# Layer 0's loop: the second layer's modulation sums are written behind the second and third tile's output projection

## The chip, the cores and the metric

The kernel runs on one core of one Trainium2 chip. The metric is the device time of one execution in microseconds (us). Below, PE is the matrix engine (TensorE), DVE the vector engine, ACT the scalar engine, POOL GpSimd, and SP the engine whose queue issues nearly all the transfers (DMAs).

## What is computed

A two-layer encoder trunk over 2048 positions of 1024 features. Each layer first scales and shifts its input and, at its end, gates what the mixer made, with three vectors (shift, scale, gate) that come from a conditioning vector `c`:

```
cond = silu(c)
for layer in range(2):
    mod = cond @ ada_w[layer] + ada_b[layer]          # 1024 x 3072
    shift, scale, gate = split(mod, 3)
    h = x * (1 + scale) + shift
    y = even_mixer(h) if layer == 0 else odd_mixer(h)
    x = layer_norm(alpha * x + gate * y, ln_g, ln_b)
```

`even_mixer` (layer 0) projects `h` by `ev_w_in` to attention inputs, to the two inputs of a spatial gating unit and to a gate, runs windowed attention and the spatial gating, multiplies by the gate and projects by `ev_w_out`. `odd_mixer` (layer 1) projects by `od_w_in`, convolves, runs two gated recurrences and projects by `od_w_out`.

## The kernel before

The 2048 positions are cut into four tiles of 512 (`NT = 4`, `t` = 0 to 3). Attention comes first, for all tiles (up to about 300 us of the profile). Then a loop over the four tiles finishes layer 0 (about 300 to 900 us), and layer 1 follows. This case is about that loop.

Every product of two matrices is done in three passes: each operand is split into a rounded part and a rest (`split`, lines 154 to 156: ACT writes the rounded part, DVE subtracts), and `mm3` (lines 158 to 161) adds three matmuls. A weight unit is 128 rows by 512 columns of a weight matrix. `wunit` loads it into `raw` (three buffers, SP, line 570), ACT and DVE split it into `hl` (eight buffers, line 155 and line 156), and PE uses it for four matmuls of 512 columns in three passes, twelve in all. So the weights come down a chain SP, DMA, ACT, DVE, PE, and `hl` can run at most eight units ahead of PE. While units pass, `wunit` also calls `prepare`, which loads a piece of layer 1's weights (`praw`), splits it (`phl`) and stores it for later. The pieces of `od_w_out` are also multiplied by layer 1's gate (line 790).

One turn of the loop is:

- `sgate(t)`: four jobs of eight units, with four PSUM banks each: the first (`sv`) ends in statistics on DVE (lines 689 to 700), then the gate job, the `u` job, and a fourth whose result meets the attention output `o`. It gives `y`.
- the modulation sums that `mods` lists for this tile, by `modulation`,
- `load_hT(t + 1)`: eight transfers of 512 KB that bring the next tile's input (`ahi`, `alo`), or for the last tile `build1(0)`, which makes layer 1's first input and needs layer 1's shift and scale,
- `project_out(t, y)`: two jobs of eight units (`n` = 0 and 1). DVE multiplies each result by layer 0's gate (`gz`, line 755), adds it to `z` (line 757), and `norm_rows` normalises and stores four `z` of 128 by 1024 (lines 616 to 627).

`modulation(..., layer, part, n)` makes one half (512 columns) of one of the vectors: part 0 is shift, 1 is scale, 2 is gate. It loads four `aw` of 512 KB (line 174, two buffers), DVE multiplies and adds eight slices of 128x512 into `macc` (line 182 once and line 184 seven times), and PE then adds up the 128 partitions: for a gate by one matmul with ones (line 192), whose result ACT copies to `gate1` (line 193), for shift and scale by DVE copies into `parts` (line 202), eight matmuls of one column (line 206) and a short DVE instruction (line 211 or 213). The list is

```
mods = {0: [(0, 2, 0), (0, 2, 1)], 1: [(1, 2, 0), (1, 2, 1), (1, 0, 0)], 2: [(1, 0, 1), (1, 1, 0), (1, 1, 1)]}
```

so layer 0's own gate is summed in tile 0, layer 1's gate and half of its shift in tile 1, and the rest in tile 2. Layer 1's gate is first used when tile 3 begins, its shift and scale in `build1(0)` after tile 3's `sgate`.

The order on each engine is not the order of the text: a scheduler places the instructions, taking those that stand earlier in the program first where several are ready, and on the chip each engine then takes its own in that order. Where PE meets a matmul of line 192 or 206 whose sum is not there yet, all later matmuls wait.

Of the kernel before, what the change touches and what calls it, by code (L numbers as in the profile page):

```python
# [54 lines left out]
def kernel(  # L55
# [39 lines left out]
    def pool(stack, name, side=None, bufs=1, space=None):  # L95
        kw = {} if space is None else {"space": space}
        if side is not None:
            kw["side"] = side
        return stack.enter_context(tc.tile_pool(name=name, bufs=bufs, reuse_waits="tile", **kw))
# [63 lines left out]
    def bank(p, tag, shape=(128, C)):  # L163
        t = p.tile(list(shape), F32, tag=tag, name=tag)
        return t

    def modulation(mp, pp, tag, layer, part, n, gate=None, wide=None):
        c0 = part * D + n * C
        acc = mp.tile([128, C], F32, tag="macc", bufs=2, name="macc")
        m = mp.m  # L170
        sums = None if wide is None else bank(*pp)
        for k2 in range(KD // m):
            aw = mp.tile([128, m, C], F32, tag=tag, name="aw")
            load(out=aw, in_=ada_w[layer, k2 * m * 128:(k2 + 1) * m * 128, c0:c0 + C].rearrange(
                "(j p) n -> p j n", p=128))
            for j in range(m):
                k = m * k2 + j
                if sums is not None:
                    q = 32 * (k % 4)
                    nc.tensor.matmul(sums[q:q + 32, :], lhsT=wide[:, k], rhs=aw[:, j], start=k < 4, stop=k >= 4)  # L180
                elif k == 0:
                    ts(out=acc, in0=aw[:, j], scalar1=cond[:, 0:1], scalar2=None, op0=ALU.mult)
                else:
                    stt(out=acc, in0=aw[:, j], scalar=cond[:, k:k + 1], in1=acc, op0=ALU.mult, op1=ALU.add)
        if sums is not None:
            act(out=acc, in_=sums, func=AF.Copy)
        ps = bank(*pp)
        if part == 2:
            brow = mp.tile([1, C], F32, tag="brow", bufs=1, name="brow")
            load(out=brow, in_=ada_b[layer:layer + 1, c0:c0 + C])  # L190
            tt(out=acc[0:1, :], in0=acc[0:1, :], in1=brow, op=ALU.add)
            nc.tensor.matmul(ps, lhsT=ones, rhs=acc, start=True, stop=True)
            act(out=gate[:, n * C:n * C + C], in_=ps, func=AF.Copy)
            return
        if layer == 0:
            pr, ks = slice(0, 128), slice(4 * n, 4 * n + 4)
            parts = acc.rearrange("p (k m) -> p k m", k=4)
        else:
            pr, ks = slice(64 * n, 64 * n + 64), slice(0, 8)
            parts = mp.tile([128, 8, 64], F32, tag="parts", bufs=1, name="parts")  # L200
            for a in range(2):
                nc.vector.tensor_copy(parts[:, :, 32 * a:32 * a + 32],
                                      acc[:, 256 * a:256 * a + 256].rearrange("p (k q) -> p k q", k=8))
        w = ks.stop - ks.start
        for k in range(w):
            nc.tensor.matmul(ps[pr, k:k + 1], lhsT=parts[:, k], rhs=ones[:, 0:1], start=True, stop=True)
        dst = (shift, scale)[part][pr, layer, ks]
        v0 = layer * 24 + part * 8
        bias = vcol0[pr, v0 + ks.start:v0 + ks.stop]
        if part == 1:  # L210
            stt(out=dst, in0=ps[pr, 0:w], scalar=1.0, in1=bias, op0=ALU.add, op1=ALU.add)
        else:
            tt(out=dst, in0=ps[pr, 0:w], in1=bias, op=ALU.add)
# [310 lines left out]
    def load_hT(t):  # L524
        hT = ([], [])
        for k2 in range(4):
            hi, lo = act_pair()
            nc.sync.dma_start(out=hi.bitcast(F32), in_=h_d[t][0][:, 2 * k2:2 * k2 + 2, :])
            nc.sync.dma_start(out=lo.bitcast(F32), in_=h_d[t][1][:, 2 * k2:2 * k2 + 2, :])
            for j in range(2):  # L530
                hT[0].append(hi[:, j])
                hT[1].append(lo[:, j])
        return hT
# [24 lines left out]
    pm = pool(sp, "pm", left, bufs=2, space=PSUM)  # L558
# [8 lines left out]
    def wunit(srcs, perm=False):  # L567
        raw = tp.tile([128, C], F32, tag="raw", bufs=3, name="raw")
        for dst, src in srcs(raw):
            r = load(out=dst, in_=src)  # L570
        hl = cp.tile([128, 2, C], F32R, tag="hl", bufs=8, name="hl")
        if perm:
            v = [hl[:, i].rearrange("p (i u d) -> p i u d", u=2, i=4) for i in range(2)]
            split(v[0], v[1], raw.rearrange("p (u i d) -> p i u d", u=2, i=4))
        else:
            split(hl[:, 0], hl[:, 1], raw)
        count[0] += 1
        while todo and count[0] >= todo[0][0]:
            prepare(todo.pop(0)[1], r)
        return hl  # L580
# [23 lines left out]
    def job_tm(unit, hT, order=range(KD)):  # L604
        ps = banks()
        for i, k in enumerate(order):
            hl = unit(k)
            for b in range(4):
                sl = slice(b * 128, b * 128 + 128)
                mm3(ps[b], hT[0][k][:, sl], hT[1][k][:, sl], hl[:, 0], hl[:, 1], i == 0, i == KD - 1)  # L610
        return ps

    def norm_rows(p, z, dst, g_bc, b_bc, parts=1):
        st6 = p.tile([128, 2, 6], F32, tag="st6", bufs=2, name="st6")
        for n in range(2):
            nc.vector.bn_stats(st6[:, n, :], z[:, n * C:n * C + C])
        mv = p.tile([128, 2], F32, tag="mv", bufs=2, name="mv")
        nc.vector.bn_aggr(mv, st6.rearrange("p a b -> p (a b)"))  # L618
        rstd = p.tile([128, 1], F32, tag="rstd", bufs=2, name="rstd")
        rsqrt_eps(rstd, mv[:, 1:2], 1.0)  # L620
        w = D // parts
        for n in range(parts):
            cs = slice(n * w, n * w + w)
            zs = z[:, cs]
            stt(out=zs, in0=zs, scalar=mv[:, 0:1], in1=g_bc[:, cs], op0=ALU.subtract, op1=ALU.mult)
            stt(out=zs, in0=zs, scalar=rstd, in1=b_bc[:, cs], op0=ALU.mult, op1=ALU.add)
            store(out=dst[:, cs], in_=zs)

    sd = ExitStack()
    bp = pool(sd, "sgate", right)  # L630
# [4 lines left out]
    gates = (gate0, gate1)  # L635
# [25 lines left out]
    def out_rows(w, c0):  # L661
        def f(k):
            if k < 4:
                return lambda raw: [(raw[64 * u:64 * u + 64], w[256 * u + 64 * k:256 * u + 64 * k + 64, c0:c0 + C])
                                    for u in range(2)]
            return lambda raw: [(raw, w[k * 128:k * 128 + 128, c0:c0 + C])]
        return f
# [75 lines left out]
    def project_out(t, y):  # L743
        zt = []
        for b in range(4):
            z = bp.tile([128, D], F32, tag="z", bufs=5, name="z")
            load(out=z, in_=xs[t * C + b * 128:t * C + b * 128 + 128, :])
            zt.append(z)
        for n in range(2):
            cw = out_rows(w1, n * C)  # L750
            ps = job_tm(lambda k: wunit(cw(k)), y, (4, 5, 6, 7, 0, 1, 2, 3))
            for b in range(4):
                gz = bp.tile([128, C], F32, tag="gz", bufs=2, name="gz")
                with tc.high_priority():
                    tt(out=gz, in0=ps[b], in1=gate0[:, n * C:n * C + C], op=ALU.mult)  # L755
                zs = zt[b][:, n * C:n * C + C]
                stt(out=zs, in0=zs, scalar=ALPHA, in1=gz, op0=ALU.mult, op1=ALU.add)
        for b in range(4):
            r = t * C + b * 128
            norm_rows(bp, zt[b], x1_d[r:r + 128, :], g_bc, b_bc)  # L760
# [80 lines left out]
    mods = {0: [(0, 2, 0), (0, 2, 1)], 1: [(1, 2, 0), (1, 2, 1), (1, 0, 0)], 2: [(1, 0, 1), (1, 1, 0), (1, 1, 1)]}  # L841
    order = list(range(16, 56)) + list(range(16))
    for t, (i0, i1) in enumerate(((0, 8), (8, 24), (24, 38), (38, 56))):
        for i in range(i0, i1):
            todo.append((48 * t + 48 * (i - i0 + 1) // (i1 - i0), order[i]))
    for t in range(NT):
        y = sgate(t, hT)
        for m in mods.get(t, []):
            modulation(Ring(bp, bp, "aw", 2, 2), (pm, "pm"), "aw", *m, gate=gates[m[0]])
        hT = load_hT(t + 1) if t + 1 < NT else build1(0)  # L850
        project_out(t, y)
        if t == 0:
            vectors1()

# [6 lines left out]
    pm = pool(sa, "pm1", bufs=3, space=PSUM)  # L861
# [368 lines left out]
```

## Time and profile before

| | us |
|---|---|
| median of three runs | 1553.41 (1550.63 to 1558.35) |
| the profiled execution, time | 1552.3 |
| its span (first to last instruction) | 1550.4 |
| PE busy | 1475.9 (95%) |
| DVE busy | 1186.5 (77%) |
| ACT busy | 784.2 (51%) |

The profile gives each engine's busy time over the span, in 40 slices of 38.8 us, and can be asked for single instructions with what they waited for. 1.9 us of the profiled execution lie outside the span. PE is busy nearly throughout, so the questions are where PE stands still, and how far the chain of weight units runs ahead of it at each place.

### The profile page before, as it was taken

How to read it: one execution, taken by the hardware profiler on the slowest of the kernel's cores; microseconds unless marked ns; L12 is line 12 of the kernel's file. 1: busy time of each engine (PE TensorE's matmuls, PEld its weight loads, DVE VectorE, ACT ScalarE, POOL GpSimd, SP SyncE). 2: the span in 40 equal slices, each digit the busy share in tenths (PEclk: the TensorE clock that was granted, in tenths of full speed). 3: DMA queues.
4: the chain of work that ended last, by engine and by line, in shares of the span. 5: the costliest groups of instructions: out<-in, count | busy, mean ns of one | idle time of the engine just before them, and what ended most of it. 6: DMA issues, size and time to landing. Idle time of an engine off the chain costs nothing. (4 is left out here: it accounts for less than half of the span.)

```text
span 1550.4 us, 22105 instructions
## 1 busy us (share of the span) xinstructions
PE 1475.9 (95%) x7096; PEld 1181.1 (76%) x7096; DVE 1186.5 (77%) x2180; ACT 784.2 (51%) x1470; POOL 413.1 (27%) x496
## 2 busy tenths in 40 slices
PE   7999999989999999999999899999999999989997
PEld 3887777657777787788888777778787788877886
DVE  4499898845659576976785875878878857879996
ACT  4677777533422342243242417589498588771110
POOL 1024223212003200210030232444555513214432
PEclk9999999999999999999999999999999999999999
DMA  9367776848788979897795689797787666438862
GB/s 345 131 171 218 214 215 179 268 120 294 237 268 301 254 236 314 317 307 251 254 299 183 200 253 278 245 264 262 243 260 249 230 232 241 165 145 307 280 237 103
DMA packets 208315, 370.91 MB, mean 239 GB/s; under 512 B 55720, under 2 KB 102724, under 8 KB 208200
## 3 DMA queue, kind: packets, MB, share of 16 engines
q1 hardware_dynamic: 201192, 354.52, 70.7%
q0 software_dynamic: 7008, 14.99, 3.8%
q8 instruction: 56, 0.92, 0.2%
q14 instruction: 59, 0.48, 0.1%
HBM read 261.96 MB, written 85.97 MB: 224 GB/s over the span
## 5 line engine op out<-in xcount | busy, mean ns | idle before, releaser
L155 ACT ACTIVATE hl<-raw 128x512 fp32r<-128x512 f32 x192 | 118.7, 627 | 228.6 <-DMA raw<-in_ev_w_in_dram 136.4
L159 PE MATMUL pj<-ahi,hl 128*128 128x512 f32 x512 | 200.4, 394 | 1.1 <-DVE gz L755 1.1
L160 PE MATMUL pj<-alo,hl 128*128 128x512 f32 x512 | 201.2, 393 | 0.0
L161 PE MATMUL pj<-ahi,hl 128*128 128x512 f32 x512 | 200.2, 392 | 0.0
L156 DVE TENSOR_TENSOR hl<-raw,hl 128x512 fp32r<-128x512 f32 x192 | 131.6, 694 | 74.0 <-ACT hl L155 73.9
L151 POOL TENSOR_SCALAR rstd<-mv 128x1 f32<-128x1 f32 x32 | 32.0, 999 | 409.7 <-DVE mv L618 297.3
L159 PEld LDWEIGHTS pj<-ahi,hl 128*128 128x128 f32 x512 | 96.9, 189 | 22.2 <-DVE gz L755 1.5
L160 PEld LDWEIGHTS pj<-alo,hl 128*128 128x128 f32 x512 | 96.8, 189 | 20.5
L161 PEld LDWEIGHTS pj<-ahi,hl 128*128 128x128 f32 x512 | 96.8, 189 | 20.3
L466 POOL DMA_DIRECT2D P<-T x112 | 62.5, 566 | 177.8 <-DVE nm L431 77.6
L159 PE MATMUL pj<-wqh,hhi 128*128 128x256 f32 (+1 forms) x256 | 88.3, 349 | 2.6 <-ACT hhi L155 1.7
L431 DVE CUSTOM_DVE_ANT_0 P<-psc,mask,nsink 128x384 f32<-128x384 f32 (+1 forms) x128 | 73.7, 593 | 21.0 <-PE psc L430 20.9
L155 ACT ACTIVATE phl<-praw 128x512 fp32r<-128x512 f32 x56 | 35.4, 631 | 106.5 <-DMA praw<-in_od_w_in_dram 52.8
L160 PE MATMUL pj<-wql,hhi 128*128 128x256 f32 (+1 forms) x256 | 87.6, 343 | 0.0
L161 PE MATMUL pj<-wqh,hlo 128*128 128x512 f32 (+1 forms) x256 | 85.2, 345 | 1.1 <-DVE hlo L156 1.0
L979 DVE SCALAR_TENSOR_TENSOR ii<-ii,xc 128x1024 f32<-128x1024 f32 (+2 forms) x32 | 40.6, 1269 | 57.9 <-ACT ii L973 57.9
L434 ACT ACTIVATE P<-P,nm 128x384 f32<-128x384 f32 (+1 forms) x128 | 76.4, 601 | 11.4 <-DVE nm L431 11.2
L779 POOL TENSOR_TENSOR alo<-hm,ahi 128x512 fp32r<-128x512 f32 x32 | 48.5, 1523 | 119.1 <-DVE hm L778 115.0
L949 DVE SCALAR_TENSOR_TENSOR xc<-X,vcol,xc 128x512 f32<-128x512 f32 (+2 forms) x96 | 75.2, 817 | 0.3
L159 PE MATMUL pm<-xhi,hg 128*128 128x512 f32 (+3 forms) x160 | 55.4, 361 | 14.3 <-ACT xhi L155 6.5
L156 DVE TENSOR_TENSOR phl<-praw,phl 128x512 fp32r<-128x512 f32 x56 | 39.0, 697 | 34.2 <-ACT phl L155 23.3
L777 ACT ACTIVATE ahi<-hm,shift,scale 128x512 fp32r<-128x512 f32 x32 | 25.2, 811 | 74.4 <-DVE hm L776 67.2
(305 smaller groups left out, 4314.1 us busy)
## 6 DMA issues: line engine op xcount, KB each, us to landing
hl<-w_d SPq DMA_DIRECT2D x128, 512.0 KB, 4.7
raw<-in_ev_w_in_dram SPq DMA_DIRECT2D x128, 256.0 KB, 4.2
w_d<-phl SPq DMA_DIRECT2D x40, 512.0 KB, 4.6
aw<-in_ada_w_dram SPq DMA_DIRECT2D x32, 512.0 KB, 6.0
hg<-w_d SPq DMA_DIRECT2D x32, 512.0 KB, 5.7
P<-T SPq DMA_DIRECT2D x104, 96.0 KB, 4.7
P<-T POOLq DMA_DIRECT2D x104, 96.0 KB, 4.3
aw<-in_ada_w_dram SPq DMA_DIRECT2D x8, 1024.0 KB, 8.2
```

What stands on the lines that cost most here:

```text
L151: nc.gpsimd.tensor_scalar(out=dst, in0=src, scalar1=mul, scalar2=EPS, op0=ALU.mult, op1=ALU.add)
L155: act(out=hi, in_=src, func=AF.Copy)
L156: tt(out=lo, in0=src, in1=hi.bitcast(F32), op=ALU.subtract)
L159: nc.tensor.matmul(ps, lhsT=ahi, rhs=bhi, start=first, stop=False)
L160: nc.tensor.matmul(ps, lhsT=ahi, rhs=blo, start=False, stop=False)
L161: nc.tensor.matmul(ps, lhsT=alo, rhs=bhi, start=False, stop=last)
L431: nc.vector.tensor_tensor_reduce(out=p[:, g, 0:W], in0=ps[:, 0:W], in1=mask[:, m0:m0 + W], scale=-0.125, scalar=nsink[:, h:h + 1], op0=ALU ...
L434: act(out=p[:, g, 0:W], in_=p[:, g, 0:W], func=AF.Exp, scale=-1.0, bias=nm[:, h:h + 1], accum_out=rs[:, h:h + 1])
L466: dma.dma_start(out=pv[32 * r:32 * r + 32, 0:nb, i], in_=T[32 * i:32 * i + 32, 0:nk].rearrange("p (j r) m -> p r j m", r=4)[:, r])
L779: nc.gpsimd.tensor_tensor(out=lo[:, j], in0=h, in1=hi[:, j].bitcast(F32), op=ALU.subtract)
L949: stt(out=xc[:, w], in0=xt[:, j0 + j:j0 + j + W], scalar=vcol1[:, 8 * j + g:8 * j + g + 1], in1=xc[:, w], op0=ALU.mult, op1=ALU.add)
L979: stt(out=ii[i][:, :, w], in0=ii[i][:, :, w], scalar=1.0, in1=xc[:, None, w].to_broadcast([128, 2, W]), op0=ALU.add, op1=ALU.mult)
```

## The change

In tile 0 nothing is changed. In tiles 1 and 2 the call of `modulation` moves from between `sgate` and `load_hT` to behind `project_out`. No instruction is added or removed and no operand changes.

```
+    def later_sums(t):
+        for m in mods.get(t, []):
+            modulation(Ring(bp, bp, "aw", 2, 2), (pm, "pm"), "aw", *m, gate=gates[m[0]])
+
     for t in range(NT):
         y = sgate(t, hT)
-        for m in mods.get(t, []):
-            modulation(Ring(bp, bp, "aw", 2, 2), (pm, "pm"), "aw", *m, gate=gates[m[0]])
+        if t == 0:
+            later_sums(t)
         hT = load_hT(t + 1) if t + 1 < NT else build1(0)
         project_out(t, y)
+        if t > 0:
+            later_sums(t)
         if t == 0:
             vectors1()
```

What this does to the order on the engines, at three places. (A number behind a name tells buffers of one name apart. It differs between the two kernels for the same thing.)

PE, the second half of layer 1's gate (line 192). Before, in tile 1's `project_out`, between the first two units of its second job (banks `px`):

```order
L161 MATMUL px_6274<-hl_6280,alo_5754 128x512
L159 MATMUL px_6275<-hl_6280,ahi_5753 128x512
L160 MATMUL px_6275<-hl_6280,ahi_5753 128x512
L161 MATMUL px_6275<-hl_6280,alo_5754 128x512
L192 MATMUL pm_6031<-macc_6014,ones_138 128x512
L159 MATMUL px_6274<-hl_6297,ahi_5753 128x512
L160 MATMUL px_6274<-hl_6297,ahi_5753 128x512
```

After, near the end of the gate job of tile 2's `sgate` (banks `pja`):

```order
L159 MATMUL pja_6710<-ahi_5999,hl_6817 128x512
L160 MATMUL pja_6710<-alo_6000,hl_6817 128x512
L161 MATMUL pja_6710<-ahi_5999,hl_6817 128x512
L192 MATMUL pm_6465<-macc_6448,ones_138 128x512
L159 MATMUL pja_6711<-ahi_5999,hl_6817 128x512
L160 MATMUL pja_6711<-alo_6000,hl_6817 128x512
L161 MATMUL pja_6711<-ahi_5999,hl_6817 128x512
```

That matmul stands 267 instructions of PE later than before. The other five of lines 192 and 206 that belong to tiles 1 and 2 move back likewise. The matmul of the gate's first half now opens tile 2, while its eight slices on DVE stay where they were.

SP, tile 1, where the next tile's input is loaded. Before, two of the gate's four `aw` stand around the first `ahi` and `alo`:

```order
L174 DMA aw_6023<-in_ada_w_dram 128x2x512
L733 DMA o_7257<-o_d2_68 128x512
L733 DMA o_7266<-o_d2_68 128x512
L528 DMA ahi_6067<-h_d2_0_66 128x1024
L529 DMA alo_6068<-h_d2_1_67 128x1024
L528 DMA ahi_6071<-h_d2_0_66 128x1024
L529 DMA alo_6072<-h_d2_1_67 128x1024
L805 DMA w_d21_117<-phl_6301 128x1024
L174 DMA aw_6027<-in_ada_w_dram 128x2x512
L570 DMA raw_6338<-in_ev_w_out_dram 128x512
```

After, at the same place:

```order
L733 DMA o_7257<-o_d2_68 128x512
L528 DMA ahi_5991<-h_d2_0_66 128x1024
L529 DMA alo_5992<-h_d2_1_67 128x1024
L528 DMA ahi_5995<-h_d2_0_66 128x1024
L529 DMA alo_5996<-h_d2_1_67 128x1024
L805 DMA w_d21_117<-phl_6225 128x1024
L733 DMA o_7266<-o_d2_68 128x512
L570 DMA raw_6262<-in_ev_w_out_dram 128x512
```

The two loads are gone from here. They and the sixteen that follow them move back by some 15 to 18 weight units, into tile 2 and the start of tile 3.

DVE, the last sum (the second half of layer 1's scale). Before, it stands in tile 2's `project_out`, among the splits of its weight units:

```order
L184 SCALAR_TENSOR_TENSOR macc_7349<-aw_7354,cond_140,macc_7349 128x512
L211 SCALAR_TENSOR_TENSOR scale_144<-pm_7336,vcol0_141 64x8
L184 SCALAR_TENSOR_TENSOR macc_7349<-aw_7358,cond_140,macc_7349 128x512 x2
L156 TENSOR_TENSOR hl_7620<-raw_7618,hl_7620 128x512
L156 TENSOR_TENSOR hl_7637<-raw_7635,hl_7637 128x512
L156 TENSOR_TENSOR phl_7641<-praw_7640,phl_7641 128x512
L184 SCALAR_TENSOR_TENSOR macc_7349<-aw_7362,cond_140,macc_7349 128x512 x2
```

After, it stands in the first job of tile 3's `sgate`, among `norm_rows` of tile 2, the statistics of `sv` and the multiplications by `gate1`:

```order
L184 SCALAR_TENSOR_TENSOR macc_7764<-aw_7773,cond_140,macc_7764 128x512
L690 TENSOR_SCALAR mu_7955<-mu_7955 128x8
L690 TENSOR_SCALAR mu_7967<-mu_7967 128x8
L626 SCALAR_TENSOR_TENSOR z_7311<-z_7311,rstd_7698,b_bc_4083 128x1024
L156 TENSOR_TENSOR hl_8143<-raw_8141,hl_8143 128x512
L790 TENSOR_TENSOR praw_8146<-praw_8146,gate1_4085 128x512
L184 SCALAR_TENSOR_TENSOR macc_7764<-aw_7777,cond_140,macc_7764 128x512
L694 TENSOR_TENSOR sv_7958<-pja_7794,mu_7955 128x512
L694 TENSOR_TENSOR sv_7970<-pja_7795,mu_7967 128x512
L790 TENSOR_TENSOR praw_8195<-praw_8195,gate1_4085 128x512
L184 SCALAR_TENSOR_TENSOR macc_7764<-aw_7777,cond_140,macc_7764 128x512
```

All eight slices of that sum, and the copies of two sums into `parts`, now lie between the `gz` of tile 2's second job and the end of tile 3's statistics. The order on POOL is the same in both kernels.

## The prediction

> **What bounds the kernel now.** First the page: span, busy times, and the slices of PE and DVE.
>
> ```profile
> span 1550.4 us, 22105 instructions
> ...
> PE 1475.9 (95%) x7096; PEld 1181.1 (76%) x7096; DVE 1186.5 (77%) x2180; ACT 784.2 (51%) x1470; POOL 413.1 (27%) x496
> ...
> PE   7999999989999999999999899999999999989997
> ...
> DVE  4499898845659576976785875878878857879996
> ```
>
> PE is the bound, with 74.5 us idle in the whole span. A change of order can win only where PE waits, and lose only by new waits. So next I cut the loop that is changed into windows of 20 us. The columns are PE, weight loads, DVE, ACT, POOL (busy us, count), granted clock, DMA share, GB/s.
>
> ```profile
> core 0: us, PE busy (x) PEld busy (x) DVE busy (x) ACT busy (x) POOL busy (x), PEclk, DMA share, GB/s
> ...
> 580.00:600.00 20.00, 16.77 (x66) 12.78 (x65) 11.03 (x19) 3.88 (x7) 0.00 (x0) 0.91 1.00 311
> 600.00:620.00 20.00, 20.00 (x101) 16.46 (x100) 15.92 (x27) 4.95 (x9) 0.00 (x0) 1.00 0.96 319
> 620.00:640.00 20.00, 20.00 (x90) 16.56 (x89) 20.00 (x34) 5.87 (x10) 5.88 (x8) 1.00 0.78 274
> 640.00:660.00 20.00, 18.32 (x81) 14.88 (x80) 20.00 (x36) 6.89 (x12) 4.48 (x5) 1.00 1.02 365
> ...
> 740.00:760.00 20.00, 20.00 (x90) 16.56 (x89) 12.90 (x23) 5.99 (x10) 0.00 (x0) 1.00 0.91 323
> 760.00:780.00 20.00, 20.00 (x90) 16.55 (x89) 20.00 (x33) 6.22 (x10) 6.77 (x7) 1.00 0.62 209
> 780.00:800.00 20.00, 20.00 (x90) 16.57 (x89) 17.89 (x30) 7.28 (x13) 7.29 (x10) 1.00 0.95 320
> 800.00:820.00 20.00, 20.00 (x90) 16.58 (x89) 13.27 (x21) 9.59 (x17) 1.33 (x1) 1.00 0.77 255
> ```
>
> Two windows lose PE time. At 580 to 600 the DMA engines are full (1.00) and the clock drops. At 640 to 660 PE loses 1.7 us, and DVE is full from 620 on. From 760 on DVE is full too, yet PE is not held up there. Third, the timeline of PE gives the waits one by one (in brackets: idle time, and what ended it).
>
> ```profile
> 444.34 1.10 PE L192 MATMUL pm<-macc,ones 128*128 128x512 f32 x2 [2.49 <-DVE macc L191]
> 592.79 1.81 PE L192 MATMUL pm<-macc,ones 128*128 128x512 f32 x2 [3.23 <-DVE macc L191]
> 648.36 0.73 PE L161 MATMUL pjb<-ahi,hl 128*128 128x512 f32 x2 [1.68 <-DVE hl L156]
> ...
> 854.47 0.50 PE L159 MATMUL pja<-hl,ahi 128*128 128x512 f32 x1 [0.88 <-ACT yt L736]
> 877.86 0.50 PE L159 MATMUL pjb<-hl,ahi 128*128 128x512 f32 x1 [1.57 <-DVE gz L755]
> 881.56 0.50 PE L159 MATMUL pjb<-hl,ahi 128*128 128x512 f32 x1 [1.59 <-DVE gz L755]
> 901.05 0.50 PE L159 MATMUL pj<-ahi,hl 128*128 128x512 f32 x1 [1.06 <-DVE gz L755]
> ```
>
> The wait of 444 belongs to tile 0 and stays. The one of 592.79 is the second half of layer 1's gate, which the change moves. Its cause, from the timelines of SP and DVE:
>
> ```profile
> 576.15 0.42 SPq L528 DMA_DIRECT2D ahi<-h_d  x1
> ...
> 579.35 0.66 SPq L174 DMA_DIRECT2D aw<-in_ada_w_dram  x1
> ...
> 581.97 0.74 DVE L184 SCALAR_TENSOR_TENSOR macc<-aw,cond,macc 128x512 f32<-128x512 f32 x1
> 589.25 1.54 DVE L184 SCALAR_TENSOR_TENSOR macc<-aw,cond,macc 128x512 f32<-128x512 f32 x2 [6.54 <-DMA aw<-in_ada_w_dram]
> 591.97 0.67 DVE L191 TENSOR_TENSOR macc<-macc,brow 1x512 f32<-1x512 f32 x1
> ```
>
> The last `aw` of this sum was issued behind the burst of `ahi` and `alo` and took 9.9 us (579.35 to 589.25). DVE stood still for it and for the splits queued behind it, and PE for DVE.
>
> **The change part by part.**
>
> *The wait at 592.79 goes.* It cost more than its 3.23 us: behind it the clock was halved.
>
> ```profile
> 593.00:596.40 3.40, 3.40 (x7) 2.03 (x7) 1.58 (x4) 1.12 (x2) 0.00 (x0) 0.51 1.01 268
> ...
> 445.00:449.00 4.00, 4.00 (x19) 3.12 (x18) 4.00 (x8) 0.59 (x1) 0.00 (x0) 1.00 0.88 275
> ```
>
> 3.40 us at 0.51 lose 3.40 x 0.49 = 1.7 us. After the 2.49 us at 444 the clock stayed at 1.00. So the term is 3.23 + 1.7 = 4.9 us. Without this matmul PE has `hl` units in store there (it was a sum that was missing, no weight unit), and two loads of 512 KB leave the burst. What would be late next is the weights of the same burst: they get earlier, not later.
>
> The Trainium skill, page "TensorE: Matmul & The Clock Gate", section "Part 1: The HAM clock gate", has the clock go to half only after an idle window of about 3.4 us, and the window running free. Read strictly, a gap of 3.23 us holds no whole window; the row of 593 shows that here it sufficed, so the trace disagrees by a little. By the strict rule the term would be 3.23 and the end result 1.7 us later.
>
> *The wait at 648.36 goes for the most part.* It is a weight unit that DVE split too late, some 28 us into the stage in which it is full. What one sum costs DVE, by the instructions on `macc` (duration in ns: least, median, most):
>
> ```profile
> L184 DVE SCALAR_TENSOR_TENSOR macc<-aw,cond,macc x56: 684/746/753, 365.6 to 732.1; 128x512 f32<-128x512 f32 x56
> L182 DVE TENSOR_SCALAR macc<-aw,cond x8: 468/474/485, 364.6 to 714.7; 128x512 f32<-128x512 f32 x8
> ...
> L202 DVE COPY parts<-macc x8: 271/285/295, 617.3 to 733.6; 128x256 f32<-128x256 f32 x8
> ```
>
> And the landing of the `aw` that are issued between 560 and 740 us:
>
> ```profile
> DMA to landing us min/median/max: 3.8/5.4/9.8
> ```
>
> One sum is 0.47 + 7 x 0.746 = 5.7 us, a pair of copies 0.57. Between 600 and 620 a whole sum with its copies leaves DVE (6.3 us, and 2 MB of loads at a DMA share of 0.96). Between 620 and 650 the slices of one sum are replaced by those of another, so the load stays. DVE enters this stage further ahead, but PE comes 4.9 us earlier. Bounds 0 and 1.68; I take 1.2, near the full wait, as the relief of 6.3 us is above the 4.9.
>
> *The six moved matmul places.* Each can hold up PE, bounded by 0 and by the 4.9 us of the worst seen. The gate's first half: its slices on DVE do not move and its matmul now stands 192 instructions of PE later (some 43 us at 90 in 20.00 us), so 0. The second half comes near the end of tile 2's gate job, shift's first half a few units later, each but a few units behind the DVE rows that it needs, while DMA is at 1.02 (640 to 660). The others have a whole job between. I take 1.2 us in all, nearer to 0, since in the loop two of eight such sums waited.
>
> *Tile 3's first job.* DVE gets one sum (5.7), two pairs of copies (1.1) and three short ones (0.3): 7.1 us in a stage that is full. What lies between DVE and PE there: the subtraction of the first job's last unit and its first matmul, and the same for the third job's first unit.
>
> ```profile
> 785.35 0.68 DVE L156 TENSOR_TENSOR hl<-raw,hl 128x512 fp32r<-128x512 f32 x1
> ...
> 793.06 0.68 DVE L694 TENSOR_TENSOR sv<-px,mu 128x512 f32<-128x512 f32 x1
> ...
> 794.66 1.37 DVE L156 TENSOR_TENSOR hl<-raw,hl 128x512 fp32r<-128x512 f32 x2 [0.32 <-ACT hl L155]
> ...
> 789.26 0.39 PE L159 MATMUL pjb<-ahi,hl 128*128 128x512 f32 x1
> ...
> 801.50 0.39 PE L159 MATMUL px<-ahi,hl 128*128 128x512 f32 x1
> ```
>
> The first lead is 789.26 - 786.03 = 3.2 us. Ahead of that subtraction six slices and a pair of copies are put (0.47 + 5 x 0.746 + 0.57 = 4.8), so the unit is 1.6 us late. The second lead is 801.50 - 795.35 = 6.2, against 7.1: 0.9 late, which the first wait already covers. The last `sv` ends at 793.7 + 7.1 = 800.8, in time for the banks at 801.50. DVE may enter further ahead, since the sum has left 715 to 733; but at 740 to 760 it is only 12.90 busy, so it is not what limits the lead, and I count nothing for that. Bounds 0 and 7.1; I take 1.5. Behind it DVE recovers, having 6.7 us free in 800 to 820.
>
> *No cost:* ACT's two copies of the gate move behind matmuls that are earlier in PE's order than the units ACT splits then; with 51% ACT has room. The loads are the same bytes, and the moved ones end before `build1(0)`. Layer 1's order does not change.
>
> Sum: -4.9 - 1.2 + 1.2 + 1.5 = -3.4 us. Against the profiled execution's 1552.3 that is 1548.9. The median of the runs lies 1.1 above that execution, so I predict 1550.
>
> **The rivals.**
>
> *The waits only change place* (the change then does not do what it says: the sums still fall among other matmuls, a third of a tile later). One moved matmul waits as at 592.79, 4.9 us again, beside tile 3's 1.5: 1552.3 - 1.2 + 1.5 = 1552.6, 1553.7 on the median. For it: DMA at 1.02 in 640 to 660, where the second half's loads now fall. Against: the six waited once before, and now most have a job between.
>
> *All waits of the tail close:* the two named (6.6 us) and the four from 854 to 901 (0.88 + 1.57 + 1.59 + 1.06 = 5.1): -11.7, which gives 1540.6, or 1541.7 on the median. For it: PE arrives earlier at them. Against: they are ended by `gz` and `yt`, which follow PE's own results.
>
> *Slower: the last sum's loads come late in tile 3's first job.* DVE takes its instructions in order, and DMA is at 0.95 in 780 to 800. If both its later loads hold DVE as at 589.25, the units are late by 7.1 + 2 x 6.54 - 3.2 = 17.0 us, 18.7 with a slow clock. With the gains of 6.1 that is +12.6: 1564.9, or 1566 on the median. It decides from a lateness of about 6 us on (the gains), and is slower by a measurable amount from 14 us on. Against it: the loads are issued some 5 units ahead of their use, and the median took 5.4 us to land.
>
> **How the numbers follow.** 0.5% is 7.8 us, about what a measurement of this kernel can tell from no change: faster means below 1545.6, slower above 1561.2. The forecast, 1546 to 1553, has a chance of 0.58; the waits that change place, 1552 to 1558, 0.25; all waits closed 0.10; late loads 0.07. Faster is the third case, 0.10. Slower is most of the last, 0.06. The rest, 0.84, cannot be told from no change. The range runs from 1544 (both named waits gone and nothing new, 6.6 us, less a little) to 1558 (the second case, with as much as the highest run shown).
>
> **What would show it.** After: line 192 without a wait near 590 and a clock of 1.00 in 580 to 600; no wait near 648; DVE at 20.00 through 760 to 800, and a wait of 1 to 3 us of PE near 790 ended by `hl` or `sv`. I am wrong if a matmul of line 192 or 206 waits over 3 us at its new place, if DVE waits for `aw` near 790, or if layer 1 takes a different time.

## The result, and the profile after

| | before | after |
|---|---|---|
| median of 17 runs | 1552.56 us | 1561.61 us |
| lowest to highest | 1546.79 to 1560.18 | 1555.81 to 1571.41 |
| the profiled execution, time | 1552.3 | 1563.16 |
| its span | 1550.4 | 1561.4 |

The ratio of after to before is 1.0051, with a 95% interval of 1.0037 to 1.0065. The change makes the kernel slower by some 8 us, where the prediction had 1550 us and called a difference too small to tell the likeliest outcome. The means of the 17 runs, 1561.2 and 1553.2 us, are 8.0 us apart. One run of one kernel below (the new place with neither loads nor wide slices), at a granted clock of 0.848 and 1631.59 us, is left out of its ratio.

The page of the changed kernel, the lines that answer to those of before:

```profile
span 1561.4 us, 22109 instructions
...
PE 1483.7 (95%) x7096; PEld 1184.9 (76%) x7096; DVE 1186.6 (76%) x2180; ACT 782.5 (50%) x1470; POOL 417.7 (27%) x496
...
PE   7899999899999998999999999999999999989997
```

PE has the same number of matmuls and is busy 7.8 us longer (1483.7 against 1475.9). A matmul at half clock counts as busy for longer (0.63 us instead of 0.39 behind the wait near 593 before), so a part of the loss must be granted clock. The other engines do as many instructions in nearly the same time (POOL 417.7 us against 413.1). The four instructions more in all (22109 against 22105) are semaphore waits, which count on no engine. The windows of 20 us over the changed loop show where it falls (columns as before: PE, weight loads, DVE, ACT, POOL, granted clock, DMA share, GB/s):

```profile
580.00:600.00 20.00, 15.83 (x63) 12.33 (x63) 8.54 (x15) 5.13 (x9) 0.00 (x0) 0.91 0.80 253
600.00:620.00 20.00, 19.17 (x83) 15.18 (x81) 7.65 (x14) 4.82 (x9) 0.00 (x0) 1.00 0.84 275
620.00:640.00 20.00, 19.35 (x85) 15.91 (x86) 20.00 (x34) 5.05 (x9) 5.41 (x6) 1.00 0.61 193
640.00:660.00 20.00, 19.53 (x85) 15.11 (x83) 18.76 (x32) 6.35 (x12) 4.38 (x7) 1.00 1.01 361
740.00:760.00 20.00, 17.11 (x70) 13.72 (x69) 12.04 (x20) 5.83 (x10) 0.00 (x0) 0.91 0.85 279
...
800.00:820.00 20.00, 19.15 (x88) 15.68 (x89) 17.68 (x34) 10.10 (x19) 7.35 (x8) 0.91 0.69 218
```

The window of 580 to 600 did not get better: PE 15.83 us busy instead of 16.77, the clock again 0.91. The one of 640 to 660 did (19.53 instead of 18.32). New losses stand at 740 to 760 and 800 to 820, both with a clock of 0.91, where PE had been full and the clock 1.00. Smaller ones, at full clock, stand at 600 to 640, at 660 to 700 and at 780 to 800. DVE was busy for 11.03 and 15.92 us between 580 and 620 and is now busy for 8.54 and 7.65, as the sum is gone from there, and PE gains nothing from it. The timeline of PE names the waits:

```profile
594.16 0.50 PE L159 MATMUL pjb<-hl,ahi 128*128 128x512 f32 x1 [3.29 <-DVE gz L755]
596.47 0.80 PE L159 MATMUL pjb<-hl,ahi 128*128 128x512 f32 x1 [0.88 <-DVE gz L755]
620.65 0.50 PE L159 MATMUL px<-hl,ahi 128*128 128x512 f32 x1 [1.48 <-DVE gz L755]
649.86 0.73 PE L161 MATMUL pjb<-ahi,hl 128*128 128x512 f32 x2 [0.38 <-DVE hl L156]
678.31 1.09 PE L206 MATMUL pm<-ones,parts 128*64 128x1 f32 x16 [0.78 <-DVE parts L202]
697.13 1.09 PE L719 MATMUL pm<-wsT,sv 128*64 128x128 f32 x16 [1.43 <-DVE yt L722]
743.29 0.80 PE L159 MATMUL pjb<-hl,ahi 128*128 128x512 f32 x1 [2.89 <-DVE gz L755]
798.89 0.73 PE L161 MATMUL pjb<-ahi,hl 128*128 128x512 f32 x2 [0.70 <-DVE hl L156]
800.85 0.77 PE L159 MATMUL pja<-ahi,hl 128*128 128x512 f32 x1 [1.22 <-DVE sv L694]
```

**Near 590** line 192 no longer waits, and in its place PE waits for `gz`, which frees a PSUM bank (3.29 and 0.88 us). `gz` itself waits for nothing that PE owes it. It stands on DVE behind splits of weights that were not there. SP, ACT and DVE in turn:

```profile
575.52 0.38 SPq L528 DMA_DIRECT2D ahi<-h_d  x1
...
579.23 2.59 SPq L570 DMA_DIRECT2D raw<-in_ev_w_out_dram  x3
...
589.50 1.16 ACT L155 ACTIVATE hl<-raw 128x512 fp32r<-128x512 f32 x2 [10.14 <-DMA raw<-in_ev_w_out_dram]
...
590.16 1.29 DVE L156 TENSOR_TENSOR hl<-raw,hl 128x512 fp32r<-128x512 f32 x2 [9.76 <-ACT hl L155]
...
593.42 0.68 DVE L755 TENSOR_TENSOR gz<-pjb,gate 128x512 f32<-128x512 f32 x1
```

The four loads of `ahi` and `alo` go ahead of three loads of weights. ACT stands for these 10.14 us, DVE for ACT 9.76 us, and `gz`, which comes behind four splits on DVE, starts at 593.42, 17.9 us after the burst began. Before, the sum's matmul stood first in PE's order and hid this second wait: there `gz` started 17.0 us after the burst (576.15), hardly sooner:

```profile
593.18 0.67 DVE L755 TENSOR_TENSOR gz<-pjb,gate 128x512 f32<-128x512 f32 x1
```

So two chains led to the same stretch of PE, and one was taken away.

**Near 740** the same thing happens one tile later, where it did not before. First the kernel before: the burst on SP, `gz` on DVE, the matmul of PE that needs `gz`, and two of the sums' matmuls that stood on PE in between:

```profile
716.98 0.42 SPq L528 DMA_DIRECT2D ahi<-h_d  x1
...
735.29 0.68 DVE L755 TENSOR_TENSOR gz<-pjb,gate 128x512 f32<-128x512 f32 x1
...
737.55 0.39 PE L159 MATMUL pjb<-hl,ahi 128*128 128x512 f32 x1
...
717.71 1.09 PE L206 MATMUL pm<-ones,parts 128*64 128x1 f32 x16
...
736.19 1.09 PE L206 MATMUL pm<-ones,parts 128*64 128x1 f32 x16
```

Then the changed kernel, DVE ahead of the burst, SP, and ACT and DVE behind it:

```profile
720.28 0.69 DVE L156 TENSOR_TENSOR hl<-raw,hl 128x512 fp32r<-128x512 f32 x1 [3.26 <-ACT hl L155]
...
723.61 0.69 DVE L737 TENSOR_TENSOR yt<-yt,o 128x512 f32<-128x512 f32 x1
...
713.85 0.37 SPq L174 DMA_DIRECT2D aw<-in_ada_w_dram  x1
...
724.33 0.32 SPq L733 DMA_DIRECT2D o<-o_d  x1
724.74 0.56 SPq L528 DMA_DIRECT2D ahi<-h_d  x1
...
736.10 0.63 ACT L155 ACTIVATE hl<-raw 128x512 fp32r<-128x512 f32 x1 [9.05 <-DMA raw<-in_ev_w_out_dram]
...
742.55 0.68 DVE L755 TENSOR_TENSOR gz<-pjb,gate 128x512 f32<-128x512 f32 x1
```

From the burst to `gz` it takes about as long in both: 735.29 - 716.98 = 18.3 us before, 17.8 after. What changed is when PE comes for it. Before, PE reached that matmul 737.55 - 716.98 = 20.6 us after the burst and did not wait. After, it was ready at 743.29 - 2.89 = 740.40, which is 15.7 us after the burst, and waited 2.89 us. The burst begins later against PE's work: five `aw` (697.05 to 713.85) now stand among the weight loads ahead of it on SP, where one stood before (716.51), DVE waits 3.26 us for a weight unit, the last `yt` comes at 723.61, and the last load of `o` and the burst stand behind it on SP. And PE comes sooner, as it has no matmuls of line 206 to do on the way (2 x 1.09 us).

The store of split weights differs too around the start of the burst. ACT, before and after:

```profile
721.57 0.63 ACT L155 ACTIVATE hl<-raw 128x512 fp32r<-128x512 f32 x1 [3.31 <-PE pja L161]
...
719.61 0.63 ACT L155 ACTIVATE hl<-raw 128x512 fp32r<-128x512 f32 x1 [3.32 <-DMA raw<-in_ev_w_out_dram]
```

Before, ACT waits for PE to free an `hl`, so the units are as far ahead as the buffers allow; after, it waits for a weight load.

The clock halves behind these waits, for 3.4 us each (windows over the first matmuls behind them):

```profile
743.00:746.40 3.40, 3.11 (x8) 2.48 (x9) 2.04 (x4) 0.58 (x2) 0.00 (x0) 0.54 0.89 246
...
800.80:804.20 3.40, 3.35 (x8) 2.73 (x9) 3.40 (x6) 1.81 (x4) 0.00 (x0) 0.51 0.92 293
```

Over all runs, count (1 - granted clock) x span as the time lost to the clock. It is 25.4 us in the mean of the changed kernel's 17 runs and 22.0 to 22.5 us in the means of the kernel before beside the first eleven experiments (95 runs in all, mean times 1553.1 to 1553.6). So of the 8.0 us about 3 go with the clock, and the other 5 are left for waits. This is an attribution and no measurement, since time lost to the clock need not reach the end. In the two profiled executions it can be followed by counting PE's matmuls in order (those of lines 159 to 161, 180 and 430): because of more half clock before 360 us, where the two programs are the same, the changed kernel is 3.4 us behind at 379 us (382.4 against 379.0), yet 0.5 us ahead at 584 (583.9 against 584.4). From there it falls behind: by 13.2 us at 806 (819.2), 11.6 at 908 (919.6) and 11.0 at 1531 (1542.0). The loss arises between 584 and 806 us.

### The profile page after: what moved, and what is told of

The parts are those of the page before. It is cut to its first block, busy times and chain, and to the rows that moved or that the text cites. A ratio compares the mean times of both kernels' runs of the same rounds, so it can differ in the third digit from the quotient of the medians.

```text
span 1561.4 us, 22109 instructions
## 1 busy us (share of the span) xinstructions
PE 1483.7 (95%) x7096; PEld 1184.9 (76%) x7096; DVE 1186.6 (76%) x2180; ACT 782.5 (50%) x1470; POOL 417.7 (27%) x496
## 5 line engine op out<-in xcount | busy, mean ns | idle before, releaser
L434 ACT ACTIVATE P<-P,nm 128x384 f32<-128x384 f32 (+1 forms) x128 | 76.5, 602 | 12.7 <-DVE nm L431 12.1
L955 DVE SCALAR_TENSOR_TENSOR xc<-X,vcol,xc 128x512 f32<-128x512 f32 (+2 forms) x96 | 78.5, 853 | 0.3
L974 ACT ACTIVATE ra<-pm,vcol 128x512 f32<-128x512 f32 (+2 forms) x80 | 47.3, 605 | 29.4 <-PE pm L161 29.1
```

The costliest lines, as they stand in the source:

```text
L434: act(out=p[:, g, 0:W], in_=p[:, g, 0:W], func=AF.Exp, scale=-1.0, bias=nm[:, h:h + 1], accum_out=rs[:, h:h + 1])
L955: stt(out=xc[:, w], in0=xt[:, j0 + j:j0 + j + W], scalar=vcol1[:, 8 * j + g:8 * j + g + 1], in1=xc[:, w], op0=ALU.mult, op1=ALU.add)
L974: r = act(out=ra[i][:, e, p0:p0 + n], in_=p[:, 0:n], func=AF.Sigmoid, bias=vcol1[:, 40 + q:41 + q])
```

## The experiments

Every kernel but the last was timed in 8 or 12 runs beside the kernel before on the same chip, whose median there was 1553.2 to 1553.5 us; a ratio is to it, with a 95% interval. Since one kernel's runs are spread over some 13 us (above), no single run decides anything here, and a profile shows one run: that of tile 1 alone below is the fastest of its kernel (1554.07 us), as is that of the spread burst in the kernel before (1553.90), and that of the narrow slices at the new place is the slowest (1561.48).

**The change for one tile alone.** First only tile 1's three sums are moved:

```
-        if t == 0:
+        if t != 1:
             later_sums(t)
...
-        if t > 0:
+        if t == 1:
             later_sums(t)
```

> Only tile 1's three sums stand behind the projection; tile 2's stand where they stood before. Two theories of the 8 us that the change costs. Loads: the aw loads that now fall among tile 2's weight units take DMA and queue time from them, the splits' lead shrinks, and the burst of the next tile's input then leaves PE waiting for gz in tile 2's projection. Tile 3: DVE gets the last sum in a stage that is full already. Here the loads are as in the change up to the last sum, and tile 3 as before. Loads expects a wait of about 3 us of PE for gz in tile 2's projection, with a slow clock, and a time 4 to 7 us above before. Tile 3 expects no more than 1 us above before.

And only tile 2's (`t != 2` and `t == 2`):

> Only tile 2's sums stand behind the projection; tile 1's stand where they stood before. The loads among tile 2's weight units are then as before, and only the last sum (loads, slices, copies) goes to tile 3, with the matmuls of the last three. Loads expects no wait for gz in tile 2's projection and a time within 2 us of before. Tile 3 expects PE waits of 2 us and a slow clock near 800 us, and 4 to 6 us above before.

Measured: tile 1 alone 1559.69 us, 1.0048 [1.0028, 1.0069]; tile 2 alone 1557.71 us, 1.0033 [1.0015, 1.0051]. Each half costs nearly as much as the whole, so the price is no sum of two parts. With tile 1 alone PE waits for `gz` near 590 as in the changed kernel (4.01 us), and near 740 for a sum whose slices come late (2.52 us, line 206). With tile 2 alone the wait of line 192 near 590 is there as before (3.75 us). So taking the gate's sum out of tile 1 removes line 192's wait and puts one for `gz` there, with or without the rest of the change.

Neither theory has both kernels. Loads had the time of the first right, but its wait for `gz` near 740 did not come; there the wait is for a sum, with half clock behind it. Of the second it had the missing wait for `gz` near 740 right and the time, within 2 us of before, wrong. Tile 3 had the time of the second right and that of the first wrong; of its 2 us of waits near 800 with half clock, PE shows 1.22 us for `sv` (790.77) at full clock. What the 4.5 us of the second kernel consist of stays open.

**Only the end of the sums moved.** In the kernel before, loads and slices stay where they stood in the program, and only what follows the slices (the bias row, PE's matmul, the copy) is written behind the projection, for tile 1's second half of the gate and first half of the shift:

```
+        late = []
         for m in mods.get(t, []):
-            modulation(..., *m, gate=gates[m[0]])
+            modulation(..., *m, gate=gates[m[0]], late=late if m in ((1, 2, 1), (1, 0, 0)) else None)
         hT = load_hT(t + 1) if t + 1 < NT else build1(0)
         project_out(t, y)
+        for end in late:
+            end()
```

> The kernel before, with tile 1's loads and slices of the gate's second half where they were, and only what follows the slices (bias, matmul, copy) of the gate's second half and of shift's first half written behind the projection; the later sums move a few units back with it. The prediction's reading (PE was held up by that matmul alone) expects no PE wait near 592 and a time 3 to 5 us below before. The burst theory expects PE to wait there for gz in its stead, 3 us and more, and a time within 3 us of before.

Measured: 1556.03 us, 1.0029 [1.0013, 1.0046]. This takes that matmul away from there and leaves the loads and slices of its sum where they were on SP and DVE (those of the shift come later than before):

```profile
593.95 0.50 PE L159 MATMUL pjb<-hl,ahi 128*128 128x512 f32 x1 [2.04 <-DVE gz L762]
596.62 0.50 PE L159 MATMUL pjb<-hl,ahi 128*128 128x512 f32 x1 [0.99 <-DVE gz L762]
```

3.03 us of the 3.23 come back as waits for `gz` (without a half clock, in this execution). It shows directly that a second chain ended in the same stretch. Near 619 a wait of 1.09 us for `gz` is new, near 649 1.36 us of the 1.68 are left, and the kernel is slower, where the prediction's reading had 3 to 5 us less.

**The burst spread out.** If the four loads ahead of the weights are the cause, they should be ordered one by one between the weight loads. Here each of the eight waits for the weight load of its own unit:

```
-        hT = load_hT(t + 1) if t + 1 < NT else build1(0)
+        hT = queue_hT(t + 1) if t + 1 < NT else build1(0)
...
+        for u, (k2, i) in zip((10, ..., 17), [(k2, i) for k2 in range(4) for i in range(2)]):
+            nextin.append((48 * (t - 1) + 33 + u, lambda pred, k2=k2, i=i: one(k2, i, pred)))
```

In the changed kernel:

> The change, and in every tile the eight transfers of the next tile's input (ahi, alo) are ordered one by one behind the weight loads of the projection, where before four of them went out together; the loads of aw stay where the change has them. If the waits for gz in the projections (3.3 and 0.9 us near 594, 2.9 near 743) come from splits that the burst makes late, with gz queued behind them on DVE, they go here with their two slow clocks, and the time falls by 6 to 11 us below that of the change, to before or up to 2 us below it. The rival, that gz is late because of the sums that were moved, expects them to stay and a time of 6 to 9 us above before.

In the kernel before:

> The kernel before with the same spreading of the next tile's input; the sums stay in their old places. The burst theory expects the wait near 592 (3.2 us and a slow clock) to shrink to under 1.5 us, and a time 2 to 6 us below before. The rival, that the gate's matmul alone held PE up there, expects the wait to stay unless its own aw lands earlier, and a time within 2 us of before.

Measured: 1560.22 us, 1.0045 [1.0025, 1.0065], and 1559.39 us, 1.0035 [1.0017, 1.0052]. Both expectations of the time failed. The remedy works where it was aimed at and pays elsewhere. PE in the changed kernel with the spread loads:

```profile
542.20 0.50 PE L159 MATMUL px<-ahi,hl 128*128 128x512 f32 x1 [3.50 <-DVE gu L733]
...
593.72 0.50 PE L159 MATMUL pjb<-hl,ahi 128*128 128x512 f32 x1 [0.90 <-DVE gz L775]
...
738.96 0.79 PE L159 MATMUL pjb<-hl,ahi 128*128 128x512 f32 x1 [3.36 <-DVE gz L775]
```

Near 594 the 4.17 us are down to 0.90. But a wait of 3.50 us near 542 (0.91 in the changed kernel), a longer one near 740 and a half clock of 10.2 us there take it back. In the kernel before with the spread loads the wait of line 192 is gone, but PE waits 1.73 us for `gz` at 592.46 and 2.88 us for it at 617.09, where it did not wait before. So near 590 the burst makes `gz` late in the changed kernel, but spreading it is no gain.

**What the sums cost at the new place, and at the old.** Four kernels leave out part of the sums of tiles 1 and 2, at the old place and at the new. Either the 20 loads of `aw` are left out (the slices read a tile that is in the buffer already), or seven of eight slices are cut to 32 of 512 columns, or both:

```
-            aw = mp.tile([128, m, C], F32, tag=tag, name="aw")
-            load(out=aw, in_=ada_w[...])
+            aw = g_bc.rearrange("p (j n) -> p j n", j=2)
...
-            stt(out=acc, in0=aw[:, j], ..., in1=acc, ...)
+            stt(out=acc[:, 0:32], in0=aw[:, j, 0:32], ..., in1=acc[:, 0:32], ...)
```

The change without its loads, and with narrow slices:

> The change, but the sums of tiles 1 and 2 are made of a tile that lies in SBUF (the row of layer 0's norm weights) and none of their aw is loaded: the loads are left out, DVE's slices and the matmuls stay, so that the output is not the reference's. Loads expects the wait in tile 2's projection to go and a time at or up to 4 us below before. Tile 3 expects the waits near 800 us to stay, where the last sum still falls there, and a time 3 to 5 us above before.

> The change, but in tiles 1 and 2 seven of the eight slices of each sum are only 32 columns wide on DVE (part of the sum is left out): all loads stay. Loads expects most of the loss to stay, 3 to 6 us above before, with the wait for gz in tile 2's projection. Tile 3 expects the waits near 800 us to go and a time within 3 us of before.

Then the same at the old place, and both together at either:

> The kernel before, its sums of tiles 1 and 2 at their old place, their slices read from a tile that lies in the buffer anyway, so that their 20 loads of 512 KB are left out (the sums are not the reference's). At the new place leaving out the same loads saved 5.9 us (1561.2 to 1555.3). Theory 1, the loads cost more at the new place than at the old one: here leaving them out saves less than 3 us, 1550 to 1553, ratio 0.998 to 1.000. Theory 2, they cost the same at either place and the loss of the change lies in the order of the other instructions: 1546 to 1548, ratio about 0.996, so that the change without loads is again some 8 us above the kernel before without loads.

> The kernel before, with seven of the eight slices of each sum of tiles 1 and 2 cut to 32 columns (the sums are not the reference's), so that DVE is relieved of most of their work at the old place. At the new place that saved 5.6 us (1561.2 to 1555.6). Theory 1, DVE's work costs more at the new place: here it saves less than 3 us, 1550 to 1553. Theory 2, it costs the same at either place: 1546 to 1548, ratio about 0.996.

> The kernel before with neither the loads nor seven eighths of the slices of the sums of tiles 1 and 2 (the sums are not the reference's): what is left at the old place is the order and the short matmuls. Theory 1: these sums cost the kernel before little, at most the waits of 592.79 and 648.36 with the half clock, 6.6 us: 1546 to 1552. Theory 2 says nothing of its level, only that the next kernel is 8 us above it.

> The change with neither the loads nor seven eighths of the slices of the moved sums (the sums are not the reference's): the moved matmuls and the order of the program are all that is left of it. Theory 1, the loss of the change is the loads together with DVE's slices at the new place: within 2 us of the kernel before without both, both near 1546 to 1552. Theory 2, it is the order (the places of the matmuls): 7 to 9 us above the kernel before without both.

Measured:

| sums of tiles 1 and 2 | old place | new place |
|---|---|---|
| whole | 1552.56 us | 1561.61 us, 1.0051 [1.0037, 1.0065] |
| without loads | 1557.90, 1.0027 [1.0006, 1.0049] | 1555.31, 1.0013 [0.9989, 1.0038] |
| narrow slices | 1556.64, 1.0016 [0.9999, 1.0033] | 1555.58, 1.0016 [0.9998, 1.0034] |
| neither | 1553.65, 1.0003 [0.9983, 1.0023] | 1552.23, 0.9983 [0.9962, 1.0004] |

Read along a line, the new place costs 9.05 us with whole sums, and -2.6, -1.1 and -1.4 us with a part of them left out (by the ratios -0.1, 0.0 and -0.2%, each with some 0.3% to either side; the two middle lines were timed on different chips at the two places). The second theory had 8 us in every line; it falls. The order of the program and the places of the short matmuls cost nothing that can be told here. It takes the loads and the slices together, and leaving out either is enough. So neither theory of the first four kernels holds alone: Loads had most of the loss stay with narrow slices, and Tile 3 had 3 to 5 us stay without loads.

Read down a column, leaving everything out is worth 9.4 us at the new place and nothing at the old one. The first theory had 1550 to 1553 for the two kernels in the middle of the old place; they came out at 1557.9 and 1556.6, above the kernel before although they do less. It had the last line within 2 us of each other, which is right, and both at 1546 to 1552, a little too low. Leaving loads out also moves other instructions (the order is planned anew), so a few us of any single number in this table may be that: without loads at the old place PE waits 3.23 us for `gz` at 619.97, with half clock for 6.8 us from there, where the kernel before has neither. The firmest contrast is that of the first and the last line at the new place, whose intervals lie well apart.

How the two remedies work is seen near 740. Without loads, the burst on SP, the first `gz` on DVE, and PE:

```profile
715.00 0.38 SPq L531 DMA_DIRECT2D ahi<-h_d  x1
...
732.13 0.68 DVE L758 TENSOR_TENSOR gz<-pjb,gate 128x512 f32<-128x512 f32 x1
...
732.87 0.50 PE L159 MATMUL pjb<-hl,ahi 128*128 128x512 f32 x1
...
735.61 0.50 PE L159 MATMUL pjb<-hl,ahi 128*128 128x512 f32 x1 [1.31 <-DVE gz L758]
```

and with narrow slices:

```profile
723.79 0.38 SPq L529 DMA_DIRECT2D ahi<-h_d  x1
...
739.08 0.69 DVE L756 TENSOR_TENSOR gz<-pjb,gate 128x512 f32<-128x512 f32 x1
...
740.31 0.39 PE L159 MATMUL pjb<-hl,ahi 128*128 128x512 f32 x1
...
741.85 0.50 PE L159 MATMUL pjb<-hl,ahi 128*128 128x512 f32 x1 [0.24 <-DVE gz L756]
```

Without loads PE comes later against the burst (732.87 - 715.00 = 17.9 us instead of 15.7); with narrow slices `gz` comes sooner (739.08 - 723.79 = 15.3 us instead of 17.8). Of the 2.89 us of wait, 1.31 and 0.24 are left, and the granted clock is 1.00 from 720 to 760 in both. What makes `gz` sooner or PE later is read off one execution each and not tested further. Near 800 the picture is another: without loads PE waits 0.96 us for `hl` at 790.09 and 2.42 us for `sv` at 793.24, more than in the changed kernel, though at full clock.

The kernel before without both has no wait of line 192 near 590 and none near 648, the two that the prediction took for gains, and yet takes the time of the kernel before. PE in it:

```profile
588.73 1.09 PE L210 MATMUL pm<-ones,parts 128*64 128x1 f32 x16 [0.90 <-DVE parts L206]
592.84 0.50 PE L159 MATMUL pjb<-hl,ahi 128*128 128x512 f32 x1 [0.40 <-DVE gz L759]
...
662.00 0.50 PE L159 MATMUL pjb<-ahi,hl 128*128 128x512 f32 x1 [2.04 <-ACT gu L712]
...
827.36 0.50 PE L159 MATMUL px<-ahi,hl 128*128 128x512 f32 x1 [2.11 <-DVE gu L717]
```

The 4.9 us of the two waits are 1.3 here, and 2.04 and 2.11 us have appeared where PE was not held up before. At the new place without both, PE still waits 2.51 us for `gz` at 590.01 with half clock behind it, so that wait needs none of the moved loads and slices; near 740 0.61 us are left.

**The changed kernel, profiled again.**

> The changed kernel, profiled a second time, to see which of its waits belong to the kernel and which to one execution. Theory 1, the waits come from the order and the loads: PE again waits for gz near 594 (2.5 to 4.5 us in all), near 620 (1 to 2), near 743 (2 to 4) and for hl and sv near 800 (1.5 to 2.5), with half clock behind two or more of them, though not always the same ones. Theory 2, the waits are chance of one execution: one of 743 and 800 is missing or under half its size.

Measured: 1561.62 us in one run (the kernel before beside it 1557.10). The waits are the kernel's, not one execution's:

```profile
594.09 0.50 PE L159 MATMUL pjb<-hl,ahi 128*128 128x512 f32 x1 [2.75 <-DVE gz L755]
...
742.28 0.80 PE L159 MATMUL pjb<-hl,ahi 128*128 128x512 f32 x1 [2.69 <-DVE gz L755]
...
799.91 0.76 PE L159 MATMUL pja<-ahi,hl 128*128 128x512 f32 x1 [1.22 <-DVE sv L694]
```

All three are within 0.6 us of the first profile's, the clock is halved for 3.4 us at 595, 742 and 800, and only the wait near 619 (0.84 us) is under what was expected of it.

No kernel tried here beats the kernel before by more than its interval. And every other kernel that does the whole work (five besides the change: each tile alone, the late ends, the spread burst twice) is slower than it by 0.3 to 0.5%. So a part of the 8 us may be the price of leaving an order that happened to fit, whatever is moved; no run here separates that from the price of the new place.

## Why the prediction was wrong, point by point

- **"The wait at 592.79 goes" (-4.9): wrong, and here the prediction failed.** The step is its last sentence, "What would be late next is the weights of the same burst: they get earlier, not later." The burst lost two loads, and its weights still held ACT for 10.14 us, and `gz` stands behind them on DVE. PE did not lack weight units there, as foretold; what it lacked was a PSUM bank that `gz` had to free. The place cost 3.23 + 1.7 = 4.9 us before and 3.29 + 0.88 + 1.7 = 5.9 after (the clock of 580 to 600 is 0.91 in both): +1.0 instead of -4.9.
- **"The wait at 648.36 goes for the most part" (-1.2): right.** 0.38 us are left of 1.68, so -1.3. It is the only gain that came.
- **"The six moved matmul places" (+1.2): about right.** Lines 192 and 206 wait 0.78 us once (678.31). A wait of 1.43 us for `yt` at 697.13 is new and was in no term.
- **"Tile 3's first job" (+1.5): the mechanism was right, the size not.** PE waits for `hl` as foretold (0.70 us) and for `sv` (1.22), which the sum had in time; the 1.9 us together are near the term, but the half clock behind them adds 1.7, which it left out.
- **"No cost: ... The loads are the same bytes": the largest new cost.** They are the same bytes at a worse place, ahead of tile 2's burst. 2.89 us of wait and (1 - 0.54) x 3.40 = 1.6 us of clock near 743 make 4.5 us. The step looked only at `build1(0)`, not at what stands behind the loads on SP, and it weighed the slices on DVE in tile 3 alone, not where weight units must run ahead of the burst. It is the two together: with the loads in place and narrow slices 0.24 us of the wait are left, without the loads 1.31.
- **1.48 us for `px` at 620.65** come from the late `gz` of the projection. No term had them.
- **Layer 1 takes the same time: right.** The waits of 878 to 901 are there again (1.45 and 1.63 us at 889 and 893), so the delay is passed on whole.

In sum: 1.0 - 1.3 + 0.8 + 1.4 + 3.6 + 4.5 + 1.5 = 11.5 us, less the 0.88 us at 854 that are gone: +10.6, where PE falls behind by 12.1 us between 584 and 908, the two profiled spans differ by 11.0 and the means of the runs by 8.0. The profile of the kernel before was an execution a little on the fast side in the clock (0.990; 22.2 us lost of 1553 is 0.986).

Of the rivals, "the waits only change place" had the outline and not the mechanism: it put one wait of a moved matmul beside tile 3's and came to 1553.7. The moved matmuls wait 0.78 us in all; what waits near 743 is a projection's matmul for `gz`, with half clock behind it, and the wait near 590 stayed where it was. The rival for a slower kernel named `aw` that come late in tile 3's first job; no DVE instruction waits for `aw` there. The chance for slower, 0.06, rested on that one mechanism alone. None of the three signs of being wrong came, since none looked at `gz`; of the signs of being right, the clock of 580 to 600 (0.91 instead of 1.00) and DVE at 760 to 780 (17.23 instead of 20.00) failed.

On the clock the Trainium skill, page "TensorE: Matmul & The Clock Gate", section "Part 1: The HAM clock gate", names an idle window of about 3.4 us, free-running. The rows above agree with the length of the slow pieces (3.40 us) and not with an idle time that must fill a window: the clock halved behind a wait of 2.89 us, and behind 0.70 and 1.22 us with 0.73 us of matmuls between them, while before it stayed at 1.00 behind 2.49. The clock records of the 14 traces show more: in each trace the halvings begin on one fixed grid of 3.413 us, and they follow the time that PE is idle within one cell of it (counts in the last section). The 2.49 us lie across two cells (at most 1.48 us in one); the 0.70 and 1.22 us lie in one (1.82).

## What to carry to other kernels

A wait in the trace is a gain only if nothing else ends in the same stretch: ask at each wait what is queued behind the releaser on its engine, and when that would have come. Moved loads are to be priced by what stands behind them on the queue, and by how far PE is from its next need when they go; here 15.7 us from the burst to PE was too little and 20.6 enough, as `gz` took about 18 in both. Where work left out altogether (the sums at the old place) gains nothing (1.0003 [0.9983, 1.0023]), its waits were not the bound, and such a test can be made before anything is moved.

## What the runs showed of the hardware

In all 14 traces, cut from 60 to 1530 us into the cells of their own grid of 3.413 us, every cell at full clock in which PE is idle, as the timeline has it, for more than 1.91 us is followed by half clock (78 of 78), none with less than 1.2 us is, and 26 of 148 between; this covers all 104 halvings there. So the price of a short wait, 1.7 us for each halved cell, hangs on where the wait falls on the grid: 0.70 + 1.22 us near 800 (0.75 + 1.22 the second time) paid it in both profiles of the changed kernel, while 0.96 + 2.42 us near 790 without loads (1.49 and 1.89 us in two cells) did not. And executions of one kernel on one chip were spread by 13 us (1546.79 to 1560.18) with the same instructions, more than the effect that was looked for; it took 8 to 17 runs of each to tell 0.3 to 0.5%.
